# Prologue loads, the second tile's square, the keys' copies and the last 512 columns put in another order in a hybrid decoder trunk

## The chip, the cores and the metric

The kernel runs on one core of a Trainium2 chip. The metric is device time in microseconds (us), the median of several executions. One execution of each kernel was also recorded with the hardware profiler, and the rows shown below come from that record. The engines are called PE (TensorE), ACT (ScalarE), DVE (VectorE), POOL (GpSimd) and SP (SyncE); PEld is PE's loading of weights. SP, ACT and POOL each issue DMAs.

## The reference, cut to what matters

One layer over 512 tokens of width 1024: three token mixers in parallel on the same normalised input, merged through gates, then a squared-ReLU MLP and a last normalisation. Everything is float32.

```python
h = rms_norm(x, norm_mix)
qa, ka, va, u, qm, km, vm, gates = split_in(h @ w_in)        # 1024 -> 5120 columns
ya = swa_attention(qa, ka, va, sinks, slopes) @ w_o_swa      # window 128, 8 heads, 2 key heads
ys = s5_ssm(u, lam_re, lam_im, log_step, b_*, c_*, d_skip)   # complex diagonal SSM, 512 wide
z  = gelu(ys) @ w_glu
yb = (z[..., :512] * sigmoid(z[..., 512:])) @ w_o_ssm
yc = moba_attention(qm, km, vm, slopes) @ w_o_moba           # blocks of 256, 8 heads, 2 key heads
g  = sigmoid(gates)                                          # three gates of 1024
x  = x + (g0 * ya + g1 * yb + g2 * yc) @ w_out
h  = rms_norm(x, norm_ffn)
x  = x + square(relu(h @ w_ff1)) @ w_ff2                     # 1024 -> 4096 -> 1024
return rms_norm(x, norm_final)
```

## The kernel before, in words

Activations are kept transposed, with channels on the partitions and the 512 tokens as columns. Every large product is made of three matmuls per pair of operands: each float32 operand is split into a rounded high part (a copy by ACT) and a low part (a subtraction by DVE), and high by high, high by low and low by high are summed in PSUM. So each block of weights costs a load, a cast on ACT (`high`), a subtraction on DVE (`low`) and the matmuls. The class `Stream` holds the queue of weight blocks for the first half of the kernel: `load` issues the DMA of the next block (a tile `wraw` of 512 KB), `high` and `low` split one half of a block, `take` hands the next finished half to the product.

**Order.** Each engine executes its instructions in the order in which the program writes them. In the first 27 us (the prologue) this order is written out by hand. From there until the last attention a planner interleaves the threads of the three mixers between the matmuls of `dense`: `account` keeps a clock for each engine with an assumed cost for each instruction, and `step` writes out a piece of a thread when these clocks say it is ready.

**The prologue.** The four tiles of x (128 tokens each, 512 KB) are loaded by SP, with the two tables `lam_re` and `lam_im` of the SSM (into the small tile `sm`) and the first blocks of `w_in` between them. ACT's queue loads `norm_mix` (tile `sg_`) and `log_step`. PE begins with four transposes of the identity, then transposes `sg_` into the column `gain`, then does 20 more transposes of the identity to have something to do. `norm1(t)` squares and sums a tile, takes the root and the reciprocal (`square_sum`, `rstd_of`) and scales the tile; `turn1(t)` transposes it on PE into PSUM banks that tiles 0 and 1 share, and tiles 2 and 3; `evac1(f, ...)` takes banks out of PSUM, high part by ACT and low part by DVE. PE transposes `sm` (into `pss`) for the SSM's parameters, which DVE computes in pieces (`some_params`). `first_u(w, acc, f)` is one product of 24 matmuls of 256 columns: weight block `w` (0 or 1) by the tokens of half `f` (0: tiles 0 and 1; 1: tiles 2 and 3). In the kernel before PE's order is: `turn1(0)`, `turn1(1)`, `sm`, block 0 by half 0, `turn1(2)`, `turn1(3)`, block 1 by half 0, block 0 by half 1, block 1 by half 1. Then the planned part begins with the third block.

**The keys.** `proj_k` is called twice, for the sliding window and for the blocks. For each of two key heads ACT copies the 64 rows from the PSUM tile `acc` to their own partitions and to the other 64, DVE subtracts to get the low part, and ACT copies the low part to the other partitions.

**The end.** For each token tile the last matmuls (`f2`) finish columns 0 to 511 and then 512 to 1023. After each part DVE adds the residual (`x`), ACT squares and sums, DVE multiplies by the last gain (`xg`); after the second part come root, reciprocal and the scaling of the tile, half by DVE and half by ACT, and two DMAs to the output.

Of the kernel before, what the change touches and what calls it, by code (L numbers as in the profile page):

```python
# [9 lines left out]
F32 = mybir.dt.float32  # L10
# [9 lines left out]
def trunk(ctx: ExitStack, tc: tile.TileContext, x, norm_mix, w_in, sinks, lam_re, lam_im,  # L20
# [137 lines left out]
    class Stream:  # L158
# [12 lines left out]
                for k0 in range(0, nk, 4):  # L171
                    self.jobs.append((len(self.blocks) - 1, w, k0, c0))

        def start(self, ahead=2):
            self.raw, self.nblk, self.i, self.j, self.done, self.half = {}, 0, 0, 0, [], []
            for _ in range(ahead):
                self.load()

        def load(self):
            if self.nblk < len(self.blocks):  # L180
                w, nk, c0, width = self.blocks[self.nblk]
                t = B4([128, nk, width], "wraw")
                SP.dma_start(t, w[:, c0:c0 + width].rearrange("(k p) c -> p k c", p=128))
                self.raw[self.nblk] = (t, c0)
                self.nblk += 1

# [73 lines left out]
    DVE.memset(eps, 1e-6)  # L260
    st = const.tile([128, 19], F32, name="st")
    sg_ = const.tile([8, 128], F32, name="sg_")
    ACT.dma_start(sg_, norm_mix[0].rearrange("(k p) -> k p", p=128))
    ACT.activation(st[:, 15:16], eps, AF.Sqrt)
    xt = [B8([128, 2, 1024], "x") for _ in range(2)]
# [3 lines left out]
    ACT.dma_start(lsr[64:80, :], log_step[0].rearrange("(j g) -> j g", g=2))  # L269
    for t in range(4):  # L270
        SP.dma_start(xt[t // 2][:, t % 2, :], x[0, t * 128:(t + 1) * 128, :])
        if t == 1:
            SP.dma_start(sm[16:32, :], lam_re[0].rearrange("(j g) s -> j (g s)", g=2))
            SP.dma_start(sm[32:48, :], lam_im[0].rearrange("(j g) s -> j (g s)", g=2))
            ws.start(1)
    ws.load()
    ws.load()
    ident = const.tile([128, 128], F32, name="ident")
    make_identity(nc, ident)
# [40 lines left out]
    def square_sum(t, src, sq=None):  # L320
        if sq is None:
            sq = B4([128, 1024], "sq")
        ACT.activation(sq, src, AF.Square, accum_out=st[:, t:t + 1])
        rstd_of(t)


# [204 lines left out]
    def norm1(t):  # L531
        xs = xt[t // 2][:, t % 2, :]
        square_sum(t, xs)
        DVE.tensor_scalar(xs, xs, st[:, 8 + t:9 + t], None, op0=ALU.mult)

    def turn1(t):
        xs = xt[t // 2][:, t % 2, :]
        for k in range(8):
            if t % 2 == 0 and k % 2 == 0:
                turned[t // 2, k // 2] = PS(("S", "S", "S", "O", "T", "T", "S", "S")[2 * t + k // 2],  # L540
                                            "x")
            o = (k % 2) * 256 + (t % 2) * 128
            PE.transpose(turned[t // 2, k // 2][:, o:o + 128], xs[:, k * 128:(k + 1) * 128], ident)
# [17 lines left out]
            PE.matmul(o, wk[:, 0, k % 4, :], l_, start=False, stop=False, skip_group_check=True)  # L561
            PE.matmul(o, wk[:, 1, k % 4, :], h_, start=False, stop=(k == 7), skip_group_check=True)

    norm1(0)
    turn1(0)
    norm1(1)
    DVE.tensor_copy(sm[64:80, :].rearrange("p (g s) -> p g s", g=2),
                    lsr[64:80, :].unsqueeze(2).to_broadcast([16, 2, 64]))
    params = ssm_params()
    turn1(1)  # L570
    pss = PS("T", "smt")
    PE.transpose(pss[:, 0:128], sm, ident)

# [7 lines left out]
    ws.low()  # L581
    evac1(0, (2, 3))
    norm1(2)
    DVE.tensor_copy(smt, pss[:, 0:128])
    some_params(P0)
    au = [PS("acc", "acc") for _ in range(2)]
    wu = [[ws.take(0) for _ in range(2)]]
    first_u(wu[0], au[0], 0)
    turn1(2)
    norm1(3)  # L590
    for f_ in (ws.high, ws.high, ws.low, ws.low):
        f_()
    wu.append([ws.take(0) for _ in range(2)])
    ACT.activation(st[:, 14:15], eps, AF.Silu)
    turn1(3)
    first_u(wu[1], au[1], 0)
    some_params(P1)
    evac1(1, range(4))
    for _ in range(3):
        ws.ahead()  # L600
    first_u(wu[0], au[0], 1)
# [265 lines left out]
    def proj_k(b):  # L867
        d = BR[b]
        acc = dense(h_h, h_l)
        K = d["k"] = B8([128, 2, 2, 512], "k", F32R)  # L870
        for g in range(2):
            p, o = slice(64 * g, 64 * g + 64), slice(64 - 64 * g, 128 - 64 * g)
            ACT.copy(K[p, 0, g, :], acc[p])
            ACT.copy(K[o, 0, g, :], acc[p])
            tt(K[p, 1, g, :], acc[p], K[p, 0, g, :].bitcast(F32), SUB)
            ACT.copy(K[o, 1, g, :], K[p, 1, g, :].bitcast(F32))

    def proj_v(b):
# [775 lines left out]
    for t in range(4):  # L1654
        xs = x2[t // 2][:, t % 2, :]
        s_, c_, r_ = (st[:, i + t:i + t + 1] for i in (0, 4, 8))
        xg = B4([128, 1024], "xg")
        for lo, hi in ((0, 512), (512, 1024)):
            sl = slice(lo, hi)
            for k in range(32 - LAST, 32):  # L1660
                f2(k, t, lo, hi)
            tt(xs[:, sl], bank[2 * t + lo // 512][:, lo % 512:lo % 512 + hi - lo], xs[:, sl], ADD)
            sq = B2([128, 512], "sq")
            ACT.activation(sq[:, :hi - lo], xs[:, sl], AF.Square, accum_out=s_)
            if hi < 1024:
                stt(c_, s_, 1.0 / 1024, c_ if lo else eps, MUL, ADD)
            tt(xg[:, sl], xs[:, sl], gf[:, sl], MUL)
        ACT.activation(r_, s_, AF.Sqrt, bias=c_, scale=1.0 / 1024)
        DVE.reciprocal(r_, r_)
        ts(xg[:, 0:512], xg[:, 0:512], r_, MUL)  # L1670
        ACT.mul(xg[:, 512:1024], xg[:, 512:1024], r_)
        SP.dma_start(out[0, t * 128:(t + 1) * 128, 0:512], xg[:, 0:512])
        (ACT if t == 3 else SP).dma_start(out[0, t * 128:(t + 1) * 128, 512:1024], xg[:, 512:1024])


# [28 lines left out]
```

## Time and profile before

| what | value |
|---|---|
| median of 3 runs | 798.91 us (796.45 to 800.1) |
| profiled execution | 798.28 us |
| its span on the core | 796.5 us |
| PE / DVE / ACT / POOL busy, share of the span | 97% / 74% / 55% / 12% |
| mean granted TensorE clock | 0.995 of full |

The span is the time from the first to the last thing on the core; the profiled execution lasted 1.78 us longer than its span. A row of the timeline gives start, length, engine, the line of the helper that records every operation (so always L110 or L90), operation, output and inputs; a bracket at its end says how long the engine had been idle before it and what released it. A queue name such as SPq marks the issue of a DMA, not its transfer.

### The profile page before, as it was taken

The page shows a single profiled execution, that of the slowest core. Times are in us where ns is not written, and L with a number is a line of the kernel's source. Part 1 is how long each engine was busy: PE and PEld are TensorE (multiplying, and loading weights), DVE is VectorE, ACT ScalarE, POOL GpSimd, SP SyncE. Part 2 cuts the span into 40 slices and gives each one's busy share as a digit, 9 for nine tenths or more (in the row PEclk, how much of TensorE's full clock was granted, in tenths as well). Part 3 has the DMA queues.
Part 4 walks back from the last instruction along what each step waited for, and adds up shares of the span by engine and source line. Part 5 has one row for each costly group of instructions (what it writes and reads, how often), then busy time and mean ns, then how long its engine had stood idle before and what let it go on. Part 6 is the DMA issues. An engine that isn't in the chain of part 4 may idle for free.

```text
span 796.5 us, 11554 instructions
## 1 busy us (share of the span) xinstructions
PE 773.5 (97%) x4234; PEld 662.5 (83%) x4234; DVE 589.5 (74%) x1176; ACT 440.7 (55%) x848; POOL 92.0 (12%) x140
## 2 busy tenths in 40 slices
PE   7999999989999999999999999999999999999996
PEld 6887778778888887888888888899999888888885
DVE  5885698766796588877575536888888598976774
ACT  7586733464775566653244425666666565655623
POOL 6041020040011222002212132000000000000000
PEclk9999999999999999999999999999999999999998
DMA  9352373253335789429999899733133565555702
GB/s 244 109 155 77 120 205 94 74 125 118 94 112 158 177 214 257 110 85 301 315 348 262 160 205 259 199 110 103 49 86 96 196 241 185 196 175 173 249 1 105
DMA packets 117720, 130.28 MB, mean 164 GB/s; under 512 B 5304, under 2 KB 87264, under 8 KB 117664
## 3 DMA queue, kind: packets, MB, share of 16 engines
q1 hardware_dynamic: 102544, 91.26, 37.3%
q0 software_dynamic: 14928, 38.03, 20.8%
q8 instruction: 33, 0.54, 0.3%
q10 hardware_dynamic: 192, 0.27, 0.1%
q14 instruction: 23, 0.19, 0.1%
HBM read 119.30 MB, written 37.49 MB: 197 GB/s over the span
## 4 chain that ended last, share of the span: by engine, by line
PE 81%; DVE 12%; ACT 3%; issue 2%; DMA 1%; SPq 0%; DVEq 0%; ACTq 0%
PE f L110 40%; PE acc L110 27%; PE xo L110 5%; DVE w L110 4%; DVE own L110 2%; PE s L110 2%; PE po L110 2%; PE pt L110 2%; PE y L110 1%; DVE t L110 1%; DVE pr L110 1%; PE pg L110 1%; DVE p L110 1%; DMA wraw<-in_w_in_dram 1%; ACT k L110 1%
## 5 line engine op out<-in xcount | busy, mean ns | idle before, releaser
L110 PE MATMUL acc<-hh,w 128*128 128x512 f32 (+1 forms) x672 | 215.9, 387 | 3.2 <-DVE k L110 1.9
L110 PEld LDWEIGHTS acc<-hh,w 128*128 128x128 f32 x672 | 124.8, 189 | 27.3 <-issue 3.9
L110 PE MATMUL acc<-hl,w 128*128 128x512 f32 (+1 forms) x336 | 128.5, 382 | 0.9 <-DVE hl L110 0.9
L110 PE MATMUL f<-h2h,f1w 128*128 128x256 f32 (+1 forms) x456 | 102.7, 313 | 0.2 <-ACT h2h L110 0.2
L110 DVE TENSOR_TENSOR w<-wraw,w 128x512 fp32r<-128x512 f32 x112 | 74.6, 685 | 16.3 <-ACT w L110 16.0
L110 PEld LDWEIGHTS f<-h2h,f1w 128*128 128x128 f32 x456 | 76.8, 191 | 5.6 <-ACT h2h L110 0.5
L110 PE MATMUL f<-w2s,s 128*128 128x512 f32 x336 | 79.2, 390 | 0.7 <-DVE w2s L110 0.6
L110 ACT CAST w<-wraw 128x512 fp32r<-128x512 f32 x112 | 67.3, 619 | 17.4 <-PE acc L110 8.6
L110 PEld LDWEIGHTS f<-w2s,s 128*128 128x128 f32 x336 | 62.9, 188 | 14.6 <-DVE w2s L110 1.0
L110 PEld LDWEIGHTS acc<-hl,w 128*128 128x128 f32 x336 | 63.6, 189 | 11.4 <-DVE hl L110 1.3
L110 PE MATMUL f<-h2l,f1w 128*128 128x256 f32 (+1 forms) x228 | 71.4, 313 | 0.3 <-DVE h2l L110 0.3
L110 PE MATMUL f<-xt,f1w 128*128 128x256 f32 x528 | 67.1, 283 | 0.0
L110 PEld LDWEIGHTS f<-xt,f1w 128*128 128x128 f32 x528 | 65.1, 192 | 0.1
L110 PE MATMUL acc<-o,w 128*128 128x512 f32 x192 | 47.8, 394 | 0.0
L110 ACT ACTIVATE act<-act 128x512 f32<-128x512 f32 (+1 forms) x54 | 31.8, 589 | 28.8 <-DVE act L110 27.7
L110 PEld LDWEIGHTS f<-h2l,f1w 128*128 128x128 f32 x228 | 43.5, 191 | 3.0 <-DVE h2l L110 0.5
L90 POOL DMA_DIRECT2D td<-in_w_ff_dram x42 | 36.3, 1078 | 75.6 <-DMA td<-in_w_ff_dram 74.9
L110 ACT CAST w2s<-wq 128x1024 fp32r<-128x1024 f32 x28 | 28.8, 1051 | 27.2 <-PE f L110 12.8
L110 PE MATMUL f<-w2s,av 128*128 128x512 f32 x168 | 42.6, 389 | 0.0
L90 POOL DMA_DIRECT2D g<-gb x23 | 12.8, 555 | 253.1 <-ACT gb L110 248.3
L110 DVE TENSOR_TENSOR f1w<-f1raw,f1w 128x512 fp32r<-128x512 f32 x53 | 35.9, 683 | 7.0 <-ACT f1w L110 7.0
L110 PEld LDWEIGHTS acc<-o,w 128*128 128x128 f32 x192 | 35.3, 188 | 6.8
(223 smaller groups left out, 1446.3 us busy)
## 6 DMA issues: line engine op xcount, KB each, us to landing
td<-in_w_ff_dram POOLq DMA_DIRECT2D x42, 512.0 KB, 9.5
wraw<-in_w_in_dram SPq DMA_DIRECT2D x40, 512.0 KB, 4.0
f1raw<-in_w_ff_dram SPq DMA_DIRECT2D x32, 512.0 KB, 6.3
tq<-td SPq DMA_DIRECT2D x21, 512.0 KB, 5.0
td<-td POOLq DMA_DIRECT2D x14, 512.0 KB, 10.9
wq<-in_w_ff_dram SPq DMA_DIRECT2D x14, 512.0 KB, 4.4
g<-gb POOLq DMA_DIRECT2D x23, 256.0 KB, 3.3
gl<-g SPq DMA_DIRECT2D x23, 256.0 KB, 8.1
```

What stands on the lines that cost most here:

```text
L90: return f(o, *a, **k)
L110: return f(o, *a, **k)
```

## The change

The first block of `w_in` is loaded from ACT's queue, ahead of `norm_mix`; SP's order becomes x tiles 0, 1, 2, the second block, x tile 3, `lam_re`, `lam_im`, the third block. The square of tile 1 is made by DVE (one instruction that multiplies and sums), and tiles 0 and 1 are scaled only after both squares. PE's order becomes: `turn1(0)`, `turn1(1)`, `sm`, block 0 by half 0, block 1 by half 0, `turn1(2)`, `turn1(3)`, block 0 by half 1, block 1 by half 1. The copy of `pss` and the first piece of the parameters come later on DVE. In `proj_k` the subtraction of each head is written before the second copy, and the two copies of the low parts come last. In the last token tile, columns 512 to 1023 are done in two parts of 256, and the last scaling is divided at column 640.

```diff
-        def start(self, ahead=2):
+        def start(self, eng):
             self.raw, self.nblk, self.i, self.j, self.done, self.half = {}, 0, 0, 0, [], []
-            for _ in range(ahead):
-                self.load()
-
-        def load(self):
+            self.load(eng)
+
+        def load(self, eng=None):
             if self.nblk < len(self.blocks):
                 w, nk, c0, width = self.blocks[self.nblk]
                 t = B4([128, nk, width], "wraw")
-                SP.dma_start(t, w[:, c0:c0 + width].rearrange("(k p) c -> p k c", p=128))
+                (eng or SP).dma_start(t, w[:, c0:c0 + width].rearrange("(k p) c -> p k c", p=128))
...
+    ws.start(ACT)
     ACT.dma_start(sg_, norm_mix[0].rearrange("(k p) -> k p", p=128))
     ACT.activation(st[:, 15:16], eps, AF.Sqrt)
...
     for t in range(4):
         SP.dma_start(xt[t // 2][:, t % 2, :], x[0, t * 128:(t + 1) * 128, :])
-        if t == 1:
-            SP.dma_start(sm[16:32, :], lam_re[0].rearrange("(j g) s -> j (g s)", g=2))
-            SP.dma_start(sm[32:48, :], lam_im[0].rearrange("(j g) s -> j (g s)", g=2))
-            ws.start(1)
-    ws.load()
+        if t == 2:
+            ws.load()
+    SP.dma_start(sm[16:32, :], lam_re[0].rearrange("(j g) s -> j (g s)", g=2))
+    SP.dma_start(sm[32:48, :], lam_im[0].rearrange("(j g) s -> j (g s)", g=2))
     ws.load()
...
-        ACT.activation(sq, src, AF.Square, accum_out=st[:, t:t + 1])
+        if t == 1:
+            DVE.tensor_tensor_reduce(sq, src, src, 1.0, 0.0, ALU.mult, ALU.add, st[:, t:t + 1])
+        else:
+            ACT.activation(sq, src, AF.Square, accum_out=st[:, t:t + 1])
         rstd_of(t)
...
     def norm1(t):
         xs = xt[t // 2][:, t % 2, :]
         square_sum(t, xs)
+        scaled(t)
+
+    def scaled(t):
+        xs = xt[t // 2][:, t % 2, :]
         DVE.tensor_scalar(xs, xs, st[:, 8 + t:9 + t], None, op0=ALU.mult)
...
-    norm1(0)
-    turn1(0)
-    norm1(1)
+    square_sum(0, xt[0][:, 0, :])
+    square_sum(1, xt[0][:, 1, :])
+    for t in range(2):
+        scaled(t)
+        turn1(t)
     DVE.tensor_copy(sm[64:80, :].rearrange("p (g s) -> p g s", g=2),
                     lsr[64:80, :].unsqueeze(2).to_broadcast([16, 2, 64]))
     params = ssm_params()
-    turn1(1)
     pss = PS("T", "smt")
     PE.transpose(pss[:, 0:128], sm, ident)
...
     norm1(2)
-    DVE.tensor_copy(smt, pss[:, 0:128])
-    some_params(P0)
     au = [PS("acc", "acc") for _ in range(2)]
     wu = [[ws.take(0) for _ in range(2)]]
     first_u(wu[0], au[0], 0)
-    turn1(2)
-    norm1(3)
     for f_ in (ws.high, ws.high, ws.low, ws.low):
         f_()
     wu.append([ws.take(0) for _ in range(2)])
+    norm1(3)
+    first_u(wu[1], au[1], 0)
+    turn1(2)
+    turn1(3)
     ACT.activation(st[:, 14:15], eps, AF.Silu)
-    turn1(3)
-    first_u(wu[1], au[1], 0)
+    DVE.tensor_copy(smt, pss[:, 0:128])
+    some_params(P0)
+    evac1(1, range(4))
     some_params(P1)
-    evac1(1, range(4))
...
             ACT.copy(K[p, 0, g, :], acc[p])
+            tt(K[p, 1, g, :], acc[p], K[p, 0, g, :].bitcast(F32), SUB)
             ACT.copy(K[o, 0, g, :], acc[p])
-            tt(K[p, 1, g, :], acc[p], K[p, 0, g, :].bitcast(F32), SUB)
+        for g in range(2):
+            p, o = slice(64 * g, 64 * g + 64), slice(64 - 64 * g, 128 - 64 * g)
             ACT.copy(K[o, 1, g, :], K[p, 1, g, :].bitcast(F32))
...
-        for lo, hi in ((0, 512), (512, 1024)):
+        ends = (0, 512, 1024) if t < 3 else (0, 512, 768, 1024)
+        for lo, hi in zip(ends, ends[1:]):
...
-        ts(xg[:, 0:512], xg[:, 0:512], r_, MUL)
-        ACT.mul(xg[:, 512:1024], xg[:, 512:1024], r_)
-        SP.dma_start(out[0, t * 128:(t + 1) * 128, 0:512], xg[:, 0:512])
-        (ACT if t == 3 else SP).dma_start(out[0, t * 128:(t + 1) * 128, 512:1024], xg[:, 512:1024])
+        c = 512 if t < 3 else 640
+        ts(xg[:, 0:c], xg[:, 0:c], r_, MUL)
+        ACT.mul(xg[:, c:1024], xg[:, c:1024], r_)
+        SP.dma_start(out[0, t * 128:(t + 1) * 128, 0:c], xg[:, 0:c])
+        (ACT if t == 3 else SP).dma_start(out[0, t * 128:(t + 1) * 128, c:1024], xg[:, c:1024])
```

## Rows read from the trace of the kernel before

**Rows 1.** The page: busy time, share of the span and instructions of each engine.

```profile
PE 773.5 (97%) x4234; PEld 662.5 (83%) x4234; DVE 589.5 (74%) x1176; ACT 440.7 (55%) x848; POOL 92.0 (12%) x140
```

**Rows 2.** The chain of work that ended last, 0 to 75 us: start, length.

```profile
18.30 8.79 PE acc L110 x72
...
27.11 0.59 ACT ut L110
```

**Rows 3.** Timeline, 0 to 24 us, the prologue's main instructions on their engines.

```profile
0.73 0.59 ACTq L90 DMA_DIRECT2D sg__71<-in_norm_mix_dram  x1
...
1.43 0.33 ACTq L90 DMA_DIRECT2D lsr<-in_log_step_dram  x1
...
2.41 0.18 PEld L110 LDWEIGHTS gain<-ident,sg__71 8*128 8x128 f32 x1 [0.33 <-DMA sg__71<-in_norm_mix_dram]
...
2.61 4.48 PE L110 MATMUL idle<-ident 128*128 128x128 f32 x20
...
4.41 1.06 ACT L110 ACTIVATE sq<-x 128x1024 f32<-128x1024 f32 x1 [1.55 <-DMA x<-in_x_dram]
...
7.09 1.09 PE L110 MATMUL x<-ident,x 128*128 128x128 f32 x8
...
9.57 3.02 ACT L110 ACTIVATE hh<-x,gain 128x256 fp32r<-128x256 f32 x8
...
14.53 0.28 PE L110 MATMUL acc<-hh,w 128*128 128x256 f32 x1
...
16.99 1.14 ACT L110 CAST w<-wraw 128x512 fp32r<-128x512 f32 x2 [1.67 <-DMA wraw<-in_w_in_dram]
...
20.41 3.23 DVE L110 SCALAR_TENSOR_TENSOR hl<-x,gain,hh 128x256 fp32r<-128x256 f32 x8 [1.10 <-ACT hh L110]
```

**Rows 4.** DMAs issued at 1.18, 1.43, 2.12, 2.58, 4.40 us: KB, us to landing.

```profile
x<-in_x_dram SPq DMA_DIRECT2D x1, 512.0 KB, 4.7
...
lsr<-in_log_step_dram ACTq DMA_DIRECT2D x1, 0.1 KB, 4.3
...
sm<-in_lam_im_dram SPq DMA_DIRECT2D x1, 8.0 KB, 4.3
...
wraw<-in_w_in_dram SPq DMA_DIRECT2D x1, 512.0 KB, 5.9
...
wraw<-in_w_in_dram SPq DMA_DIRECT2D x1, 512.0 KB, 12.6
```

**Rows 5.** Engines by stretch: busy us of PE, PEld, DVE, ACT, POOL; clock, DMA share, GB/s.

```profile
2.00:10.00 8.00, 7.38 (x41) 6.21 (x39) 3.08 (x7) 5.22 (x12) 7.61 (x17) 1.00 1.00 347
```

**Rows 6.** DMA traffic of two stretches, 2 to 3 and 5 to 6 us.

```profile
DMA packets 63, 0.26 MB, mean 258 GB/s; under 512 B 0, under 2 KB 0, under 8 KB 63
...
DMA packets 569, 0.29 MB, mean 291 GB/s; under 512 B 37, under 2 KB 564, under 8 KB 569
```

**Rows 7.** Groups by shape, whole span: busy us and mean ns of one, idle before.

```profile
L110 DVE CUSTOM_DVE_ANT_0 p<-s,dist_m 128x512 f32<-128x512 f32 x8 | 5.2, 684 | 0.1
...
L110 DVE TENSOR_TENSOR act<-vz,f 128x256 f32<-128x256 f32 x33 | 13.8, 418 | 6.1 <-PE f L110 5.9
...
L110 ACT ACTIVATE p<-p,nm 128x384 f32<-128x384 f32 x8 | 4.8, 607 | 0.0
```

**Rows 8.** Timeline, 137 to 145 us, around the window's keys.

```profile
142.35 1.17 ACT L110 CAST k<-acc 64x512 fp32r<-64x512 f32 x2
143.56 0.69 DVE L110 TENSOR_TENSOR k<-acc,k 64x512 fp32r<-64x512 f32 x1 [1.87 <-ACT k L110]
...
144.40 0.47 PE L110 MATMUL acc<-hh,w 128*128 128x512 f32 x1 [1.92 <-DVE k L110]
```

**Rows 9.** Timeline, 788 to 793 us, the last token tile.

```profile
788.35 0.68 DVE L110 TENSOR_TENSOR xg<-x,gf 128x512 f32<-128x512 f32 x1
789.51 0.69 DVE L110 TENSOR_TENSOR x<-f,x 128x512 f32<-128x512 f32 x1 [0.48 <-PE f L110]
...
791.64 0.72 ACT L110 ACTIVATE xg<-xg,st 128x512 f32<-128x512 f32 x1 [0.29 <-DVE st L110]
```

## The prediction, made before the changed kernel was run

> **What bounds the kernel.** I read the page's busy shares first. PE is busy for 773.5 of 796.5 us [rows 1], so little more than the 23 us in which it idles can be won, and whatever holds PE up is paid in full. Then I read the chain of waits over the first 75 us: PE's products of the prologue end at 27.09, ACT's copy of their result follows at 27.11 [rows 2], and the planned part hangs on that copy. A delay of 27.09 therefore moves everything behind it. The timeline then shows how 27.09 comes about. PE fills its time with 20 idle transposes up to 7.09, starts `turn1(0)` in that instant, and the high parts `hh` start at 9.57. The first product ends at 14.81, and from 18.30 three products run without a gap in 8.79 us, 2.93 each [rows 2, 3]. PE idles little here, because `turn1(2)`, `turn1(3)` and block 1 are done while ACT and DVE take banks out.
>
> **Loads.** Before, tile 0 is there at 4.41, tile 1 at 5.88 (1.18 + 4.7), block 0 at 8.50 (2.58 + 5.9) and block 1 at 17.0 (4.40 + 12.6; ACT's casts wait for it until 16.99) [rows 3, 4]. From 2 to 10 us DMA moves 347 GB/s [rows 5]. That is the full rate, so block 0, issued 1.9 us earlier, can only gain what others lose.
>
> I take it that the two queues share about equally. The row for this is the small `log_step` load on ACT's queue, issued at 1.43: it lands at 5.73, between tile 1 (5.88) and what was issued before it, not at once [rows 4]. Then tile 0 and block 0, 1.05 MB, are through at 2.0 + 1.05/0.347 = 5.0. In the trace block 0 has 1.59 MB up to its own end, through at 6.6, and lands at 8.50, a lag of 1.9. So block 0 now lands at about 6.9, tile 0 near 5.8, tile 1 near 7.3.
>
> `norm_mix` now stands behind block 0 in the same queue. Before, it went first (issued at 0.73) and PE's transpose into `gain` waited for it until 2.41 [rows 3]. This transpose stands on PE **ahead** of the 20 idle transposes, and they ahead of `turn1(0)`. Bounds: `norm_mix` lands at 2.4 if it isn't held up, and with block 0, at 6.9, if it is; I take 6.9, by the `log_step` row. Then gain is done at 7.2, the idle transposes take 4.48 and end at 11.7.
>
> **The second square on DVE.** It is queued behind the first tile's reciprocal. The trace has no 1024-wide one with a sum. Two nearest rows: 684 ns for the 512-wide custom instruction, and 418 for a 256-wide tensor operation [rows 7]; their slope gives 684 + 2 x 266 = 1.2, with reading the sum 1.3. Bounds: nothing, if hidden; 1.9 with the root and reciprocal that both tiles now wait for. Tile 0 is ready for `turn1(0)` at 5.8 + (7.09 - 4.41) + 1.9 = 10.4, before 11.7, so I take nothing: the idle transposes hide it. ACT's saved square (1.06) gives nothing either, since `hh` waits for PE.
>
> **The prologue, summed.** `turn1(0)` 11.7 to 12.8 (1.09), two of the eight transposes of `turn1(1)` 0.27, `hh` from 13.1 instead of 9.57: 3.5 late. The first product, paced by ACT and DVE, ends at 14.8 + 3.5 = 18.3.
>
> Ahead of it stands the transpose of `sm`, which waits for `lam_re` and `lam_im`. They landed at 6.4 (2.12 + 4.3) [rows 4] and now stand behind tile 3. With block 0, 3.15 MB are ahead of them, as were of block 1's end before, which came at 17.0; at 347 GB/s throughout and the lag of 1.9 it would be 13.0. I take 15: the first product needs them at 18.3 - 2.9 = 15.4, so nothing is added; at 17.0 it would be 1.9 more.
>
> Block 1 by half 0 needs block 1's low parts. ACT: `hh` 3.02 to 16.1, tile 2's square and root 1.5 (as 12.43 to 13.94 before), two casts 1.14 to 18.75. DVE: scaling of tile 2 to 18.8, first `low` 0.69 to 19.5. Two matmuls run ahead of that, so this product lasts from 19.25 to 22.2. Then `turn1(2)`, `turn1(3)`: 2.18, to 24.4. Only now can half 1 come out of PSUM, and no product is left to cover it. Its first bank is complete at 23.55, two high parts 0.85, eight low parts 3.23 [rows 3], to 27.6; block 0 by half 1 follows at this pace to 27.9, block 1 by half 1 takes 2.93 to 30.8. That is 30.8 - 27.1 = 3.7 late. The moved copy of `pss` and first piece of the parameters lie in DVE's idle time before 23.55, at no cost.
>
> **The keys.** PE waited 1.92 us for `acc`, released by DVE's second subtraction. But that subtraction needs only the first of two ACT copies (142.35 to 142.93) and starts at 143.56, after the second [rows 8]. So copy and subtraction, both reading `acc`, are kept apart in the order written. In the new order the second copy then waits for the subtraction: subtraction 142.97 to 143.66, copy to 144.27, which is when `acc` was free before (144.25). Gain 0; if the two may run together, up to 1.9; if the two later copies (1.2 together) hold up casts, a loss of 0.6. I take 0. The Trainium skill, "PSUM — Partial Sum Buffer", section "PSUM bank collisions raise a hardware error", says that instructions of different engines on one bank and 32-partition quadrant have to be kept apart, reads included; by that the sum has 0 here, without it -1.9. The row agrees, with its start 0.63 after the data were there.
>
> **The last columns.** PE's 24 matmuls of 256 columns take 2.93 (8.79 / 3 [rows 2]), for 12 of 512 in the 2.73 between the two parts' ends: 0.2 more. DVE is what counts. It is busy with the first part's `xg` until 789.03 [rows 9]; then add (0.42), a wait of about 0.55 for ACT's sum, `xg` (0.42) of the middle part, so the last part's add starts at about 790.5, not at 789.51. Its shorter add and square (0.27 and 0.21 less) and ACT's 384 instead of 512 columns (607 for 724 ns [rows 7, 9]) give back 0.6. Net +0.3; bounds -0.6, if the middle part were hidden, and +0.5.
>
> **Sum.** 798.28 (the profiled execution) + 3.7 + 0 + 0.3 = 802.3. The median shown is 798.91, 0.6 above that execution and inside the runs' own spread; I leave the sum as it is. A measurement of this kernel tells about 0.5% (4.0 us) from no change, so a forecast of +3.4 to +4.0 stands at that bound.
>
> **Rivals.**
> 1. *The queues alternate packet by packet.* x moves in packets of 4 KB, block 0 of 0.5 KB (0.26 MB in 63, 0.29 MB in 569 [rows 6]). For each x packet one of block 0's goes: tiles 0 to 2 pass with 24 of its 64 packets per DMA engine, the rest alternate with block 1. Then 2.43 MB are through when block 0 ends, 9.0, landing 10.9. `norm_mix` follows, the idle transposes end at 15.65, `hh` starts 3.9 later than in my sum: 806.2. For it: the packet sizes. Against: `log_step`'s small packets were not let through. The Trainium skill, "DMA: Bandwidth & Descriptors", section "Queues, rings and completion order", says that a DMA engine goes round its queues one packet at a time. It gives this rival's 806.2 if a packet is one row as the trace counts them, and my 802.3 if it is a longer group.
> 2. *The queues don't disturb each other* (not slower). `norm_mix` lands before 4.5, tile 1 as before. Then only the second square counts: `turn1(0)` at 9.0, `hh` at 10.4, 27.09 becomes 28.1 with `lam_*` at 13. 798.28 + 1.0 + 0.3 = 799.6, and 797.7 if the keys' 1.9 come off. It decides if the idle transposes end before 9. Against: 347 GB/s was already the full rate.
> 3. *`lam_re` and `lam_im` last*, landing at 17 or later: the first product ends at 20.3, half 1 at 31.8: 803.3.
> 4. *The planner.* Its clocks see other costs, so the threads may be interleaved otherwise: some 2 us either way of PE's 23 idle ones.
>
> **Chances.** Forecast with its own range 800.5 to 804: 0.45. Rival 1: 0.25. Rival 2: 0.15. Rival 3: 0.10. Rival 4 deciding: 0.05. Above 4.0 us lie nearly all of rivals 1 and 3 and some 0.4 of the forecast: slower 0.52. Faster needs rival 2 with the keys' gain and the planner's help: 0.05. Within 0.5%: 0.43. The range takes in rival 1 with the late tables, and rival 2 at its upper end: 798.8 to 807.5.
>
> **What the profile would show.** The wait of PE's `gain` transpose ends at 6 to 7 us on DMA (rival 1: 10 to 11; rival 2: before 4.5). `hh` starts near 13. A PE wait on DMA for `sm` shows only in rival 3. After `turn1(3)` PE is paced by DVE's low parts for about 3 us. ACT's copy of the first products stands near 30.8. The 1.9 us wait of PE near the window's keys is still there, now released by ACT. The last add starts after 790 from the same origin. The forecast is wrong if ACT's queue gives way to SP's or the small loads overtake, or if PE idles differently in the planned part.

## The result: 0.6% slower

The changed kernel took 804.56 us (median of 20 runs, 801.72 to 806.15), the kernel before on the same chip 799.44 (20 runs, 796.45 to 801.64). The ratio is 1.0061, with a 95% interval from 1.0048 to 1.0074. Of 799.44 that is 4.9 us (the two medians differ by 5.1), above the 0.5% (4.0 us) that was set as the bound, though the interval begins at 3.8. The forecast was 802.3 with a range from 798.8 to 807.5, and slower by over 0.5% was its likeliest case. The profiled execution took 802.78, with a span of 801.0; it is the last of a lower group of nine runs (801.72 to 802.78, mean granted clock 0.995 to 0.999), while ten lie from 805.14 to 806.15 (0.991 to 0.995) and one between them, and no trace shows an execution of the upper group.

### The profile page after: what moved, and what is told of

It reads as the page before. It is cut to its first block, busy times and chain, and to the rows that moved or that the text cites. A ratio compares the mean times of both kernels' runs of the same rounds, so it can differ in the third digit from the quotient of the medians.

```text
span 801.0 us, 11589 instructions
## 1 busy us (share of the span) xinstructions
PE 770.6 (96%) x4246; PEld 661.8 (83%) x4246; DVE 590.9 (74%) x1181; ACT 440.3 (55%) x848; POOL 92.2 (12%) x140
## 4 chain that ended last, share of the span: by engine, by line
PE 77%; DVE 13%; ACT 4%; DMA 3%; issue 2%; ACTq 0%; DVEq 0%; SPq 0%
PE f L110 35%; PE acc L110 27%; PE xo L110 5%; DVE w L110 4%; DVE own L110 3%; DMA f1raw<-in_w_ff_dram 2%; PE s L110 2%; PE po L110 2%; PE pt L110 2%; PE y L110 1%; DVE t L110 1%; DVE p L110 1%; PE pg L110 1%; DVE pr L110 1%; DMA sg__71<-in_norm_mix_dram 1%
## 6 DMA issues: line engine op xcount, KB each, us to landing
td<-td POOLq DMA_DIRECT2D x14, 512.0 KB, 10.9
```

## The profile after

The page's busy times, against [rows 1]: PE's busy time fell by 3 us while the span grew by 4.5, so PE idles more. Two terms of the loss stand out, one at each end of the kernel.

```profile
PE 770.6 (96%) x4246; PEld 661.8 (83%) x4246; DVE 590.9 (74%) x1181; ACT 440.3 (55%) x848; POOL 92.2 (12%) x140
```

**The front.** The chain of work that ended last, 0 to 75 us (start, length), against [rows 2]. It now begins with a DMA of 4 KB:

```profile
1.24 6.49 DMA sg__71<-in_norm_mix_dram
8.04 3.82 PE idle L110 x20
11.86 1.10 PE x L110 x10
12.98 3.03 ACT hh L110 x8
...
24.63 6.14 PE acc L110 x47
30.79 0.59 ACT ut L110
```

ACT's copy of the first products stands at 30.79 instead of 27.11: 3.68 late. The timeline of the same stretch, against [rows 3], gives the rest:

```profile
2.79 1.77 SPq L90 DMA_DIRECT2D x<-in_x_dram  x1
...
4.28 1.06 ACT L110 ACTIVATE sq<-x 128x1024 f32<-128x1024 f32 x1 [0.79 <-DMA x<-in_x_dram]
...
7.77 0.27 PE L110 MATMUL gain<-ident,sg__71 8*128 8x8 f32 x1 [5.28 <-DMA sg__71<-in_norm_mix_dram]
7.97 3.89 PE L110 MATMUL idle<-ident 128*128 128x128 f32 x20
8.07 0.17 DVE L110 COPY gain<-gain 128x8 f32<-128x8 f32 x1 [7.04 <-PE gain L110]
...
8.23 1.21 DVE L110 CUSTOM_DVE_ANT_0 sq<-x 128x1024 f32<-128x1024 f32 x1
8.54 0.44 SPq L90 DMA_DIRECT2D sm<-in_lam_im_dram  x1
...
11.69 1.91 PE L110 MATMUL x<-ident,x 128*128 128x128 f32 x16
12.98 3.03 ACT L110 ACTIVATE hh<-x,gain 128x256 fp32r<-128x256 f32 x8 [2.18 <-PE x L110]
...
15.60 0.30 PE L110 MATMUL smt<-ident,sm 128*128 128x128 f32 x1 [1.99 <-DVE hl L110]
...
24.09 3.23 DVE L110 SCALAR_TENSOR_TENSOR hl<-x,gain,hh 128x256 fp32r<-128x256 f32 x8 [2.28 <-ACT hh L110]
```

PE stands still for 5.28 us, until `norm_mix` has landed at 7.7 (1.24 + 6.49), little ahead of block 0; the 20 idle transposes come after it, and `hh` starts at 12.98 instead of 9.57. The row of `sm` names DVE's `hl`, but `sm` does not need it (with the tables early it is transposed ahead of `hl`, at 10.39): `lam_im` landed at 15.4 (8.54 + 6.9). The loads issued up to 6 us show the same, against [rows 4]; they end with the median us to landing:

```profile
wraw<-in_w_in_dram ACTq DMA_DIRECT2D x1, 512.0 KB, 7.3
wraw<-in_w_in_dram SPq DMA_DIRECT2D x1, 512.0 KB, 8.3
```

Block 0, issued at 0.74 and not at 2.58, is there at 8.0 instead of 8.50. Block 1, issued at 2.12, is there at 10.4 instead of 17.0, but no product could use it that early.

**The keys.** The timeline around the window's keys, against [rows 8]:

```profile
145.57 1.17 ACT L110 CAST k<-acc 64x512 fp32r<-64x512 f32 x2 [4.03 <-DVE k L110]
146.77 0.69 DVE L110 TENSOR_TENSOR k<-acc,k 64x512 fp32r<-64x512 f32 x1 [1.24 <-ACT k L110]
147.50 0.58 ACT L110 CAST k<-acc 64x512 fp32r<-64x512 f32 x1 [0.76 <-DVE k L110]
...
148.13 0.50 PE L110 MATMUL acc<-hh,w 128*128 128x512 f32 x1 [1.78 <-ACT k L110]
```

The second head's two copies and its subtraction still follow one another: the subtraction starts when the first copy has ended, the second copy (147.50) when the subtraction has ended. PE waits 1.78 instead of 1.92, now for ACT.

**The end.** The last token tile, against [rows 9]:

```profile
790.02 0.69 DVE L110 TENSOR_TENSOR x<-f,x 128x512 f32<-128x512 f32 x1 [0.16 <-PE f L110]
...
792.18 0.42 DVE L110 TENSOR_TENSOR x<-f,x 128x256 f32<-128x256 f32 x1
792.65 1.70 PE L110 MATMUL f<-w2s,as 128*128 128x256 f32 x12 [1.24 <-DVE x L110]
...
794.39 0.42 DVE L110 TENSOR_TENSOR x<-f,x 128x256 f32<-128x256 f32 x1 [0.66 <-PE f L110]
...
796.03 0.61 ACT L110 ACTIVATE xg<-xg,st 128x384 f32<-128x384 f32 x1 [0.29 <-DVE st L110]
```

From the start of the last tile's first add (790.02) to the end of ACT's last scaling (796.64) it takes 6.62. In the kernel before the first add, one part ahead of the one in [rows 9], stood in the timeline as

```profile
786.79 0.69 DVE L110 TENSOR_TENSOR x<-f,x 128x512 f32<-128x512 f32 x1 [0.17 <-PE f L110]
```

and ACT's last scaling ended at 792.36 (791.64 + 0.72 [rows 9]), 5.57 later. So this costs 1.05. From that scaling to the end of the span it takes 4.36 instead of 4.14, another 0.22.

**The sum.** 3.68 + 1.05 + 0.22 = 4.95, beside 4.9 by the ratio. That they meet is in part luck: between the two profiled executions it is only 4.50 (802.78 - 798.28), because 0.45 was given back between 31 and 790 us, and the run with the new loads alone loses more than its front shows (below). The execution before lost some time at 170 to 176, where its granted clock was 0.72; the one after did not, and instead has a wait of PE for DVE's split of the first MLP weights (`f1w`) of 1.5 near 510. Both come and go without the change: the kernel before and the three runs that differ from it in the end alone have the same code up there, and the clock falls in three of these four traces (0.66 from 170 to 175), while the wait stands in one of them (1.0).

## The experiments

The runs were timed in three groups (the first four, the next four, the last four) beside the kernel before, which had 798.89, 799.53 and 799.84. "Copy" is the start of ACT's copy of the first products (27.11 before, 30.79 after), "end" the time from the last tile's first add to the end of ACT's last scaling (5.57 before, 6.62 after).

| run | median | ratio, 95% interval | copy or end |
|---|---|---|---|
| loads only | 803.61 | 1.0067 [1.0045, 1.0088] | copy 30.02 |
| order only | 805.42 | 1.0074 [1.0048, 1.0100] | copy 33.67 |
| `norm_mix` first | 805.76 | 1.0087 [1.0054, 1.0121] | copy 31.97 |
| end only | 800.36 | 1.0022 [1.0005, 1.0038] | end 6.63 |
| `norm_mix` first, tables early | 799.60 | 1.0002 [0.9984, 1.0020] | copy 27.74 |
| keys only | 798.84 | 1.0002 [0.9981, 1.0023] | copy 26.81 |
| end, matmuls first | 800.55 | 1.0022 [1.0003, 1.0042] | end 6.59 |
| front only | 805.04 | 1.0072 [1.0043, 1.0100] | copy 30.70 |
| end, other bank | 799.99 | 1.0006 [0.9987, 1.0025] | end 5.87 |
| tables early only | 803.39 | 1.0044 [1.0021, 1.0066] | copy 31.25 |
| loads mended, old order | 800.61 | 1.0013 [0.9994, 1.0031] | copy 28.15 |
| the same, keys from SBUF | 800.36 | 1.0018 [0.9999, 1.0036] | copy 27.63 |

The copy varies with no change ahead of it: in the five traces with the front of the kernel before (that kernel, the three with a new end, the one with new keys) it stands at 26.78 to 27.98. The front's 3.68 is therefore known to about 0.6 (an estimate from these five), and so are the differences below.

**Loads only.** The kernel before with the new loads; squares, PE's order, keys and end as before.

```diff
...
+    ws.start(ACT)
     ACT.dma_start(sg_, norm_mix[0].rearrange("(k p) -> k p", p=128))
...
-        if t == 1:
-            SP.dma_start(sm[16:32, :], lam_re[0].rearrange("(j g) s -> j (g s)", g=2))
-            SP.dma_start(sm[32:48, :], lam_im[0].rearrange("(j g) s -> j (g s)", g=2))
-            ws.start(1)
-    ws.load()
+        if t == 2:
+            ws.load()
+    SP.dma_start(sm[16:32, :], lam_re[0].rearrange("(j g) s -> j (g s)", g=2))
+    SP.dma_start(sm[32:48, :], lam_im[0].rearrange("(j g) s -> j (g s)", g=2))
     ws.load()
```

> The kernel before with the loads of the change alone (block 0 from ACT's queue ahead of norm_mix, SP's new order); squares, PE's order, keys and end as before. Theory (the late norm_mix holds up the idle transposes and so everything): PE's gain transpose waits for DMA until about 7.8, hh starts near 13, sm is transposed near 15.6, ACT's copy of the block-1 product, at 27.11 before, comes near 29.6: +2.5 us, 801.9 beside 799.4. Rival (the order of PE and DVE's square cost it, the loads are hidden): that copy within 0.5 us of 27.11, time unchanged.

The copy stood at 30.02, so the loads alone cost 2.9 of the front's 3.68. PE's wait for `norm_mix` was 5.20, and `hh` started at 12.75. By the ratio the kernel lost 5.4 (3.6 to 7.0), not the 2.5 that were expected; its trace, of an execution of 799.72, does not show where the rest arises.

**Order only.** The changed kernel with the loads of the kernel before.

```diff
-    ws.start(ACT)
     ACT.dma_start(sg_, norm_mix[0].rearrange("(k p) -> k p", p=128))
...
-        if t == 2:
-            ws.load()
-    SP.dma_start(sm[16:32, :], lam_re[0].rearrange("(j g) s -> j (g s)", g=2))
-    SP.dma_start(sm[32:48, :], lam_im[0].rearrange("(j g) s -> j (g s)", g=2))
+        if t == 1:
+            SP.dma_start(sm[16:32, :], lam_re[0].rearrange("(j g) s -> j (g s)", g=2))
+            SP.dma_start(sm[32:48, :], lam_im[0].rearrange("(j g) s -> j (g s)", g=2))
+            ws.start(SP)
+    ws.load()
     ws.load()
```

> The changed kernel with the loads of before (all of them from SP, norm_mix first); DVE's square, PE's order, keys and end as changed. Theory: hh starts near 10.4, because both tiles wait for the second square; block 1 comes at 17.0 as before, so block 1 by half 0 lies idle until about 18, and half 1 then comes out of PSUM with no product to cover it: ACT's copy near 29.5, +2.4 us, plus 1.0 at the end: 802.8. So that each half of the prologue's change costs about 2.4 alone and they overlap in the 3.7 of both. Rival (only the loads cost): copy within 0.5 us of 27.11, and only the end's 1.0 is lost: 800.4.

The copy stood at 33.67, later than in the changed kernel. Block 1 by half 0 is now the next product, and its weights, loaded as before, come too late; this is the timeline of the run:

```profile
8.56 3.39 PE L110 MATMUL x<-ident,x 128*128 128x128 f32 x16 [2.55 <-DVE x L110]
...
18.88 0.58 PE L110 MATMUL acc<-hh,w 128*128 128x256 f32 x1 [2.62 <-ACT w L110]
```

After each of these two waits the granted clock is low, 0.57 from 8.5 to 12 us and 0.50 from 20 to 25. The windows of this run give the stretch, PE's busy us, then PEld, DVE, ACT, POOL, the granted clock, the DMA share and GB/s:

```profile
20.00:25.00 5.00, 5.00 (x25) 5.00 (x25) 1.96 (x8) 2.18 (x5) 0.00 (x0) 0.50 0.33 81
```

A clock of 0.50 is the lower level, 1.2 GHz. By the chain of waits this product's 24 matmuls took 5.79, and in the changed kernel 22 of them 2.89. The expectation (copy near 29.5) had not counted on that. So the new order on PE needs the early block 1, and loading it early is not in itself the mistake.

**`norm_mix` first.** The changed kernel with two lines exchanged.

```diff
-    ws.start(ACT)
     ACT.dma_start(sg_, norm_mix[0].rearrange("(k p) -> k p", p=128))
+    ws.start(ACT)
```

> The changed kernel with one line moved: norm_mix is issued on ACT's queue ahead of block 0 instead of behind it. Theory: gain is transposed before 3.5, the idle transposes end before 8, hh starts near 10, and the tables lam_re and lam_im, whose issue no longer waits for block 0 to land, come near 13.7 and set the first product; ACT's copy near 28.4: 2.4 us earlier than in the changed kernel (30.79), about 802.2 against its 804.6. Rival (the tables or DVE's square set the start, norm_mix is beside the point): ACT's copy stays within 0.5 us of 30.8 and the time that of the changed kernel.

This theory fell: the copy stood at 31.97, not at 28.4, nor near the rival's 30.8. `hh` did start early, at 10.95, but the transpose of `sm` stands ahead of the first product, and its tables `lam_re` and `lam_im` were late. The timeline and, below it, the windows of this run:

```profile
15.73 0.30 PE L110 MATMUL smt<-ident,sm 128*128 128x128 f32 x1 [3.62 <-DVE st L110]
...
31.97 0.59 ACT L110 COPY ut<-acc 128x512 f32<-128x512 f32 x1 [2.29 <-PE acc L110]
```

```profile
15.00:20.00 5.00, 4.27 (x24) 4.31 (x24) 4.48 (x13) 4.16 (x8) 1.23 (x2) 0.66 1.19 255
```

The row names a reciprocal of DVE that ended at 15.72 and that `sm` does not need; `lam_im`, issued at 4.92, took 10.7 and landed at 15.6, and in the run with the front only, where `sm`'s transpose starts at 15.00, the row names the DMA of `lam_im`. PE had been idle for 3.6 us, and the granted clock of the stretch behind it was 0.66.

**End only.** The kernel before with the new last columns.

```diff
-        for lo, hi in ((0, 512), (512, 1024)):
+        ends = (0, 512, 1024) if t < 3 else (0, 512, 768, 1024)
+        for lo, hi in zip(ends, ends[1:]):
...
+        c = 512 if t < 3 else 640
...
```

> The kernel before with the new end alone (last token tile in parts of 512, 256, 256 columns, last scaling divided at 640). Theory: PE's last 12 matmuls wait over 1 us for DVE's add on the same PSUM bank; from the first part's add of the last tile to the end of ACT's last scaling 6.6 us as in the changed kernel, against 5.57 before: +1.0 us, 800.4. Rival (as predicted, DVE's order alone costs it): 5.9 us and no such wait of PE, +0.3.

The end took 6.63, as in the changed kernel, with the same wait of PE for DVE's add (1.24); the ratio is 1.0022. So this term is independent of the front.

**`norm_mix` first and the tables early.** The new order on PE, the keys and the end stay as changed.

```diff
-    ws.start(ACT)
     ACT.dma_start(sg_, norm_mix[0].rearrange("(k p) -> k p", p=128))
+    ws.start(ACT)
...
+        if t == 1:
+            SP.dma_start(sm[16:32, :], lam_re[0].rearrange("(j g) s -> j (g s)", g=2))
+            SP.dma_start(sm[32:48, :], lam_im[0].rearrange("(j g) s -> j (g s)", g=2))
         if t == 2:
             ws.load()
-    SP.dma_start(sm[16:32, :], lam_re[0].rearrange("(j g) s -> j (g s)", g=2))
-    SP.dma_start(sm[32:48, :], lam_im[0].rearrange("(j g) s -> j (g s)", g=2))
     ws.load()
```

> The changed kernel with norm_mix issued ahead of the first block on ACT's queue and lam_re, lam_im issued behind tile 1 of x again, as in the kernel before. Theory: the front's loss has two causes of which either alone holds the first product up (norm_mix behind the block, the two tables behind everything). With both gone, PE's gain transpose runs near 3, hh starts at 10 to 11, sm's transpose at 11 to 13 and ACT's copy of the first products near 28.5 to 30, against 30.79 in the changed kernel; the end still loses its 1. Time about 800 to 802. Rival: the loss lies in the new order of PE's products and their uncovered evacuation; then the copy stands at 31 or later and TensorE's granted clock falls before 25 us, as in the run of the order alone; time about 805.

The copy stood at 27.74, earlier than the expected 28.5 to 30, and with the slower end still in it the kernel is as fast as the one before within the interval of 0.2% either way. The timeline:

```profile
3.26 0.27 PE L110 MATMUL gain<-ident,sg__71 8*128 8x8 f32 x1 [0.78 <-DMA sg__71<-in_norm_mix_dram]
...
8.59 1.97 PE L110 MATMUL x<-ident,x 128*128 128x128 f32 x16 [1.33 <-DVE x L110]
9.94 3.03 ACT L110 ACTIVATE hh<-x,gain 128x256 fp32r<-128x256 f32 x8 [1.16 <-PE x L110]
...
27.74 0.59 ACT L110 COPY ut<-acc 128x512 f32<-128x512 f32 x1 [2.29 <-PE acc L110]
```

Here, too, the square on DVE loses its cover: the idle transposes are done before tile 0 is scaled, and PE waits 1.33.

**Tables early only.** The changed kernel with `lam_re` and `lam_im` behind tile 1, `norm_mix` still behind block 0.

```diff
+        if t == 1:
+            SP.dma_start(sm[16:32, :], lam_re[0].rearrange("(j g) s -> j (g s)", g=2))
+            SP.dma_start(sm[32:48, :], lam_im[0].rearrange("(j g) s -> j (g s)", g=2))
         if t == 2:
             ws.load()
-    SP.dma_start(sm[16:32, :], lam_re[0].rearrange("(j g) s -> j (g s)", g=2))
-    SP.dma_start(sm[32:48, :], lam_im[0].rearrange("(j g) s -> j (g s)", g=2))
```

> The changed kernel with lam_re and lam_im issued behind tile 1 of x again, norm_mix still behind the first block. Theory by the run with both mended (copy at 27.74) and the one with norm_mix alone mended (31.97): each of the two alone holds the first product up, so with the tables alone mended gain still waits until about 7, hh starts near 13, sm's transpose follows turn1 at 13.5 without a wait on DMA, and ACT's copy of the first products stands at 30 to 31; the ratio is 1.004 to 1.007. Rival: the tables are the whole cause; then the copy stands near 28 and the ratio below 1.003.

The copy stood at 31.25 in the timeline of this run:

```profile
13.44 3.03 ACT L110 ACTIVATE hh<-x,gain 128x256 fp32r<-128x256 f32 x8 [2.49 <-PE x L110]
...
31.25 0.59 ACT L110 COPY ut<-acc 128x512 f32<-128x512 f32 x1 [2.29 <-PE acc L110]
```

With this run the four combinations under the new order are complete, and they fall into one pattern. Where `hh` is late, the tables add nothing: from the start of `hh` to the copy it takes 17.81 in the changed kernel (12.98 to 30.79), 17.81 here (13.44 to 31.25), and 17.80 with both loads early (9.94 to 27.74). Only where `hh` is early and the tables late is it more, 21.02 (10.95 to 31.97). Either late load alone is enough to hold up the first product.

**Front only.** The changed kernel with the keys and the end of the kernel before.

```diff
             ACT.copy(K[p, 0, g, :], acc[p])
+            ACT.copy(K[o, 0, g, :], acc[p])
             tt(K[p, 1, g, :], acc[p], K[p, 0, g, :].bitcast(F32), SUB)
-            ACT.copy(K[o, 0, g, :], acc[p])
-        for g in range(2):
...
-        ends = (0, 512, 1024) if t < 3 else (0, 512, 768, 1024)
-        for lo, hi in zip(ends, ends[1:]):
+        for lo, hi in ((0, 512), (512, 1024)):
...
```

> The changed kernel with the keys and the end of the kernel before. Theory: ACT's copy of the first products stands near 30.8 as in the changed kernel, and the time is that of the changed kernel less 1, so a ratio of about 1.004 to 1.006. Rival: the part given back between 160 and 270 us depends on the keys' order; then the time is some 1.5 us higher than that.

The copy stood at 30.70, as expected. The time was not the expected 1 less than that of the changed kernel; the ratio's interval, 1.0043 to 1.0100, is too wide for that, and leaves the rival open too.

**Keys only.**

```diff
             ACT.copy(K[p, 0, g, :], acc[p])
+            tt(K[p, 1, g, :], acc[p], K[p, 0, g, :].bitcast(F32), SUB)
             ACT.copy(K[o, 0, g, :], acc[p])
-            tt(K[p, 1, g, :], acc[p], K[p, 0, g, :].bitcast(F32), SUB)
+        for g in range(2):
+            p, o = slice(64 * g, 64 * g + 64), slice(64 - 64 * g, 128 - 64 * g)
             ACT.copy(K[o, 1, g, :], K[p, 1, g, :].bitcast(F32))
```

> The kernel before with the copies of the keys in the new order and nothing else. Theory: the second copy and the subtraction on one PSUM tile are kept apart in either order, so PE waits 1.8 to 1.9 for acc behind the window's keys as before, and the ratio is 1.000, within 0.1%. Rival: the two run together, the wait shrinks to below 1 at both calls, and the time falls by 1 to 3 us.

The ratio is 1.0002, and PE's wait for the keys 1.8. The profiled execution of this kernel took 802.35, although its runs began at 796.35. It shows one place where such a difference can arise. First PE's waits between 480 and 530 us (sum, count, longest), then the windows:

```profile
PE f L110 <- DVE f1w L110: 3.0, 2, 2.4
```

```profile
505.00:510.00 5.00, 3.02 (x12) 2.17 (x12) 3.85 (x6) 2.69 (x4) 0.00 (x0) 1.00 0.47 132
510.00:515.00 5.00, 4.37 (x14) 3.56 (x15) 4.79 (x8) 3.54 (x7) 0.00 (x0) 0.66 0.00 0
```

The `f1w` wait of the changed kernel (1.5) is here twice as long, with the old front and the old end, and the clock falls after it. Three more runs have it (1.0 with the end in another bank, 1.9 with `norm_mix` first and the tables early, 2.2 in the last run), the run with the front only has none. So this wait is not the change's; why the split comes later in some traces is open.

**The same end with all matmuls first.** PE writes the 24 matmuls of the last two parts before DVE's add reads the first of them.

```diff
...
-            for k in range(32 - LAST, 32):
-                f2(k, t, lo, hi)
+            if hi < 1024 or t < 3:
+                for k in range(32 - LAST, 32):
+                    f2(k, t, lo, hi)
+                if hi == 768:
+                    for k in range(32 - LAST, 32):
+                        f2(k, t, 768, 1024)
...
```

> The kernel before with the new end, but PE writes all 24 matmuls of the last two 256-column parts before DVE's add reads the first of them. Theory: the end's loss comes from PE's last 12 matmuls waiting 1.24 us for DVE's add on the same PSUM bank. Then that wait is gone here, and from the start of the last tile's first add to the end of ACT's last scaling it takes 5.5 to 5.9, against 5.57 in the kernel before and 6.62 in the changed one; the ratio is 0.999 to 1.001. Rival: DVE's queue sets the end whatever PE does; then 6.3 or more stay.

PE's wait was gone, and the end still took 6.59. That speaks for the rival, but the edit had put another wait in its place: the middle part's add started at 788.85, released by PE, when all 24 matmuls were done, 2.87 after the first add, and not at 2.16 as in the changed kernel (792.18 - 790.02). The run does not tell the two apart.

**The end with another bank.** The last twelve matmuls go to a PSUM bank of their own; the older sums of these columns are added to the residual one tile earlier.

```diff
...
+            if t == 2 and lo == 0:
+                tt(x2[1][:, 1, 768:], bank[7][:, 256:], x2[1][:, 1, 768:], ADD)
+            if t == 3 and lo == 768:
...
+                        PE.matmul(bank[0][:, 0:256], at[:, a_, 384:512], wt[:, w_, 768:],
...
+                tt(xs[:, sl], bank[0][:, 0:256], xs[:, sl], ADD)
...
```

> The kernel before with the new end, but the last 256 columns' twelve matmuls go to another PSUM bank; their older partial sums are added to the residual one tile earlier, which costs DVE one instruction of 0.42 away from the end. PE then need not wait for DVE's add on the middle part, nor DVE for PE's last matmul. Theory: the bank costs about 0.65 of the new end; without it the way from the last tile's first add to the end of ACT's last scaling is 5.9 to 6.0, against 6.62 in the changed kernel and 5.57 in the kernel before, and PE's wait of 1.24 is gone. Rival: DVE's queue alone sets it, and 6.5 or more stay.

Here it is told apart. The timeline has the last add at 791.44, right behind `xg`, with no wait for PE:

```profile
787.81 0.69 DVE L110 TENSOR_TENSOR x<-f,x 128x512 f32<-128x512 f32 x1 [0.16 <-PE f L110]
...
791.44 0.42 DVE L110 TENSOR_TENSOR x<-f,x 128x256 f32<-128x256 f32 x1
...
793.07 0.61 ACT L110 ACTIVATE xg<-xg,st 128x384 f32<-128x384 f32 x1 [0.29 <-DVE st L110]
```

The end takes 5.87 (787.81 to 793.68). That is the forecast's +0.3 over 5.57, and the shared bank costs the other 0.75 (a bank is also one PSUM tile of this program; the run does not tell these two apart).

**Loads mended, old order.** The kernel before with block 0 on ACT's queue behind `norm_mix`, the tables behind tile 1, and block 1 ahead of tile 3.

```diff
...
     ACT.dma_start(sg_, norm_mix[0].rearrange("(k p) -> k p", p=128))
+    ws.start(ACT)
...
-            ws.start(1)
-    ws.load()
+        if t == 2:
+            ws.load()
     ws.load()
```

> The kernel before, its squares, its order on PE, its keys and its end, with the first block on ACT's queue behind norm_mix, lam_re and lam_im behind tile 1 and the second block ahead of tile 3. Theory: block 1 lands some 5 earlier than in the kernel before, and turn1(2), turn1(3) and block 1 by half 0 still cover the evacuation of half 1, so ACT's copy of the first products stands at 26.0 to 26.8, against 27.11 in the kernel before and 27.74 with the new order on PE; the time is 0.3 to 1.1 below the kernel before, ratio 0.9985 to 1.000. Rival: ACT and DVE pace this stretch whatever is loaded when; then the copy stands at 27 to 28 and the ratio is 1.000 to 1.001.

The copy stood at 28.15, and at 27.63 in the next run, which has the same loads. With the old loads it is 26.78 to 27.98, so the expected gain of 0.3 to 1.1 is not there, and a loss is not shown. The reason is neither the theory's nor the rival's. The chain of waits begins so:

```profile
0.74 4.00 DMA x<-in_x_dram
4.74 0.02 issue
4.75 11.09 DMA x<-in_x_dram
```

SP's issue of tile 3 waited until tile 0 had landed, and tile 3 then took 11.09 behind block 1. PE waited 2.19 for it ahead of `turn1(3)`.

**The same, and the keys' second copy from SBUF.**

```diff
             ACT.copy(K[p, 0, g, :], acc[p])
-            ACT.copy(K[o, 0, g, :], acc[p])
             tt(K[p, 1, g, :], acc[p], K[p, 0, g, :].bitcast(F32), SUB)
+            ACT.copy(K[o, 0, g, :], K[p, 0, g, :].bitcast(F32))
```

> The kernel of the run before this one, and in the keys the second copy of the high part reads the first copy in SBUF instead of the PSUM tile, behind the subtraction in the program. Theory: what keeps copy and subtraction apart is that both read one PSUM tile; so here the tile is free about 0.6 a head sooner, PE's wait of 1.9 behind the window's keys shrinks to 0.7 to 1.3, and the time is 0.5 to 1.5 below that kernel. Rival: the wait is set by the first copies and the two subtractions alone, or moves to the next product; then the wait stays at 1.8 or more.

The timeline shows subtraction and ACT's copies side by side, and PE's wait falls from 1.90 in the run before to 1.32, at the edge of the expected 0.7 to 1.3:

```profile
143.49 1.35 ACT L110 CAST k<-k 64x512 fp32r<-64x512 f32 x2
143.49 0.69 DVE L110 TENSOR_TENSOR k<-acc,k 64x512 fp32r<-64x512 f32 x1 [1.28 <-ACT k L110]
144.33 0.47 PE L110 MATMUL acc<-hh,w 128*128 128x512 f32 x1 [1.32 <-DVE k L110]
```

So the new order of the keys gains nothing because both engines still read `acc`. The 0.6 us is too little to show in the time (800.36 beside 800.61). No version beat the kernel before; these keys behind the old front were not tried.

## Why the prediction was right, and where it was not

**The front, predicted +3.7, measured 3.68.** The mechanism is shown: undoing the two late loads together takes the copy back to 27.74, inside the 26.78 to 27.98 of the old front. The step on `hh` (13.1, measured 12.98) is right as a sum of two errors. The loads don't share equally: tile 0 landed at about 4.3, not at 5.8, block 0 at 8.0 and `norm_mix` at 7.7, not at 6.9, so that `gain` ended 0.8 later than 7.2. But the 20 idle transposes took 3.89 instead of 4.48. Nor was 347 GB/s the full rate, as the sum took it: the kernel before moved 409 from 7 to 8 us. Rival 1, which gives SP's larger packets more of each turn, had the right direction for the loads and the wrong size: its block 0 was to land at 10.9.

**The tables, taken as 15, measured 15.4** (8.54 + 6.9; `sm` transposed at 15.60). That SP would issue them only at 8.16 was not foreseen, but it did not set this: issued from 4.26 on, with `norm_mix` first, they landed at 15.6. The prediction's "nothing is added" is shown by the two intervals of 17.81. That this is so only because `hh` is late, it did not say.

**DVE's square, 1.3 and hidden.** It took 1.21 and 0.08 for reading the sum. It is hidden while `gain` is late; PE waits for the chain behind it 0.64 with `norm_mix` first and 1.33 with the tables early as well. The named cover was the right one.

**Half 1 uncovered.** `turn1` of tiles 2 and 3, then products at the pace of DVE's low parts to the copy at 30.79, as forecast (30.8). The order on PE itself shows no cost: 17.81 from `hh` to the copy, against 17.54 before (9.57 to 27.11) and 17.30 to 18.20 in the other four traces with the old front.

**The keys, 0.** Measured 1.0002, and the wait changed its releaser, as predicted.

**The end is the mis-sized term: +0.3 predicted, 1.05 measured, 1.27 to the end of the span.** The step that failed is "the last part's add starts at about 790.5", 3.7 after the first add. It started 4.37 after it. The sum counted DVE's queue and ACT's sums, which alone give 5.87, with the last add 3.63 after the first, as the run with another bank shows, but it let PE's last twelve matmuls run through. They had to wait for the middle part's add, because both parts lie in one bank. The Trainium skill, "PSUM — Partial Sum Buffer", section "PSUM bank collisions raise a hardware error", says that a PE write and a reader on one bank and quadrant have to be kept apart. The prediction weighed this rule for the keys and left it out here, where it bore on PE too; the trace agrees with it in both places (0 at the keys, 0.75 here).

**The base.** 798.28 was the sum's base, and the 20 runs of the kernel before have the median 799.44. That is 1.2 of the 2.3 between 802.3 and 804.56; the end is 1.0 of it. The profiled execution of the changed kernel, 802.78, lies 0.5 above the forecast: 1.0 more at the end, 0.45 less between 31 and 790 us. So that execution lies nearer to the forecast than the terms warrant, by luck.

**The planner, rival 4.** In the two traces it did not decide: 2.2 were given back between 31 and 419 us (the `xo` matmuls of the chain start at 419.04, before at 417.57), and 1.8 lost by the first add of the last tile. Part of both comes from the clock's fall and the `f1w` wait, which come and go. How much of the rest is the planner's is open.

## What to carry to other kernels

Before a big load is put ahead of a small one in a queue, look for what waits for the small one: here a load of 4 KB held PE for 5.28 us, and behind it stood filler work that was meant to run during the wait. Where two late inputs hold up one stretch, mending one may show nothing (31.97 and 31.25 here, beside 27.74 with both), so mend both before a theory is dropped. When the reading of a product out of PSUM is cut into smaller parts, look at which banks they lie in: here PE waited 1.24 us for DVE while two parts shared a bank, and not at all when they did not.

## What was unexpected in the hardware's rows

- A load's issue can wait for the landing of an unrelated load. In the changed kernel SP issued `lam_re` at 8.16, when block 0 of ACT's queue had landed (the row below, sum, count and longest of SP's waits up to 30 us). Why it waits for that load no trace shows. In the kernel with the mended loads this befell tile 3, which was issued at 4.75, when tile 0 had landed.

```profile
SPq L90 <- DMA wraw<-in_w_in_dram: 3.5, 1, 3.5
```

- The first tile of x on SP's queue was not disturbed by block 0 on ACT's queue: ACT's square of tile 0 starts at 4.28, before at 4.41 [rows 3], while block 0 took 7.3 and the 4 KB behind it 6.5. The second tile was: with the new loads only, where ACT squares it too, the timeline has ACT waiting for it until 7.09. Before it was there at 5.88; the prediction's 7.3 was near.

```profile
7.09 1.06 ACT L110 ACTIVATE sq<-x 128x1024 f32<-128x1024 f32 x1 [1.40 <-DMA x<-in_x_dram]
```

- Idle time of PE in the prologue can be paid twice. In the run of the order only the granted clock was 0.57 from 8.5 to 12 us, behind a wait of 2.55 us, and 0.50 from 20 to 25, behind one of 2.62, and a product that takes 2.9 took 5.8; with `norm_mix` first it was 0.66 behind a wait of 3.6. After the 5.28 us in the changed kernel the rows of the clock give 1.00 (7.77 to 12 us), but the rows of the matmuls do not fit that: the idle transposes that start up to 9.7 took 421 to 475 ns each, as `turn1` does in the run of the order only at 0.57 (421 in the median), while `turn1` of the changed kernel, the same instruction, took 272. At which level PE ran there is open.
